# A batched matmul with scale and add: transposes moved from the matmul engine to three other engines, and a new order of transfers

## The chip, the cores and the metric

The kernel runs on one core of a Trainium2 chip. The metric is the device time of one execution in microseconds (us); the times shown are medians over several executions. One execution was also recorded by the hardware profiler: a page with summary tables and a trace of single instructions and transfers.

The engines are named as the profile names them: PE is TensorE (matmuls; PEld is its weight load), DVE is VectorE, ACT is ScalarE, POOL is GpSimd, SP is SyncE, which here only issues DMA transfers.

## The reference

```python
batch, m, k, n = 16, 512, 1024, 768
x: [16, 512, 1024] f32    weight: [1024, 768] f32    scale: 0.1    add_value: [16, 512, 768] f32
return (scale * np.matmul(x, weight) + add_value).astype(np.float32)
```

The batch is flattened: x has M = 8192 rows of K = 1024, the output 8192 rows of N = 768. The matmul is done in bf16 with f32 sums.

## The kernel before, in words

**Tiles.** The 8192 rows are cut into T = 64 tiles of 128 rows. Eight tiles form a group, so that one transfer brings several tiles at once in long runs: row p*8+t of a group is tile t, partition p. The weight (3.1 MB) is kept in SBUF as w_bf, 8 slices of 128 rows of K.

**Buffers.** x lands in xs, a ring of 16 tiles in f32. add_value lands in ao, a ring of 32 tiles; the result of a tile overwrites its addend there, and is sent out from there. The last eight slots of ao first hold the raw weight, and three below them the first three products until their addends come.

**The work on a tile.** The matmul needs x with K on the partitions, that is transposed. A tile is cast to bf16, and two neighbouring bf16 values are treated as one f32, so that four 128x128 f32 blocks are turned instead of eight. The rows of the weight are laid out to suit: slice 2c and 2c+1 hold the even and odd rows of a block. In the kernel before there are two ways to turn a tile:

- On PE (44 tiles): POOL casts the tile into an xb buffer (cast_to), PE turns the four blocks into PSUM (transpose, four matmuls with an identity), ACT copies them to an xt buffer in SBUF and separates even from odd.
- On DVE (20 tiles, the ten pairs of PAIRS): POOL casts both tiles of a pair into vx (cast_pair); DVE turns 32x32 blocks from one group of 32 partitions to another into vt (turn_pair), 16 instructions a pair, four after each of four steps.

Then product() issues 16 matmuls a tile: eight weight loads of 128x128 from the turned tile, each for 512 and for 256 columns. finish() on DVE multiplies by the scale, adds the addend and writes into ao.

**The order.** All is written out by hand; manual_schedule() keeps the order of the program on each engine. The list STREAM names the transfers in the order in which SP issues them: "x", "w" and "a" are loads, "o" stores; each entry has the first tile and the number of tiles. Ahead of a load into used slots of xs, or of a store, the program runs step() until the tiles concerned have been handed on. SP waits at each entry for the semaphores of what used the slots before, and later entries wait behind it. All transfers go through one queue to 16 DMA engines. In what follows x(16) means the entry that starts with tile 16 of x.

**The head.** The first three tiles are multiplied slice by slice as the weight arrives (head). Ten matmuls on zeros (WARM) are issued before.

**The steady state.** step() takes one tile t: its first eight matmuls, then the transposes of tile t+1 on PE, the cast of tile t+AHEAD, and the cast of a pair that starts at t+7; then the other eight matmuls, finish(t), and the DVE turns of the pair that starts up to six tiles ahead. The last tile is done in two parts, 512 columns and then 256.

Of the kernel before, what the change touches and what calls it, by code (L numbers as in the profile page):

```python
# [10 lines left out]

STREAM = [
# [6 lines left out]
]  # L19

X_SLOTS = 16
A_SLOTS = 32
AHEAD = 6
EARLY = 3
WARM = 10


PAIRS = [14, 19, 24, 29, 34, 39, 44, 49, 54, 59]


@with_exitstack
def kernel(
# [8 lines left out]
    nc = tc.nc  # L41
    P = 128
    bf16 = mybir.dt.bfloat16
    fp32 = mybir.dt.float32
# [4 lines left out]
    M, K = x_f.shape  # L49
    _, N = weight.shape  # L50
    T = M // P

    KC = K // (2 * P)
    KJ = 2 * KC
    CUT = 512
# [4 lines left out]
    out_v = out_f.rearrange("(g p t) n -> p g t n", p=P, t=G)  # L60

    def rows(view, s, n):
        assert s // G == (s + n - 1) // G
        return view[:, s // G, s % G:s % G + n, :]


    w_v = weight.rearrange("(c p r) n -> p c r n", p=P, r=2)

    const = ctx.enter_context(tc.tile_pool(name="const", bufs=1))
    xb_pool = ctx.enter_context(tc.tile_pool(name="xb_pool", bufs=7))  # L70
    xt_pool = ctx.enter_context(tc.tile_pool(name="xt_pool", bufs=EARLY + 1))
    vx_pool = ctx.enter_context(tc.tile_pool(name="vx_pool", bufs=1))
    vt_pool = ctx.enter_context(tc.tile_pool(name="vt_pool", bufs=2))
    tp_pool = ctx.enter_context(
        tc.tile_pool(name="tp_pool", bufs=2, space=bass.MemoryType.PSUM))
    mm_pool = ctx.enter_context(
        tc.tile_pool(name="mm_pool", bufs=3, space=bass.MemoryType.PSUM))
    ctx.enter_context(tc.manual_schedule())

    zeros = const.tile([P, CUT], bf16, name="zeros")  # L80
    nc.vector.memset(zeros, 0.0)  # L81
    identity = const.tile([P, P], fp32, name="identity")
    make_identity(nc, identity)
    xs = const.tile([P, X_SLOTS, K], fp32, name="xs")
    ao = const.tile([P, A_SLOTS, N], fp32, name="ao")
    w_bf = const.tile([P, KJ, N], bf16, name="w_bf")

    xb_tiles, xt_tiles, mm_tiles, done = {}, {}, {}, {"cast": 0, "step": 0, "x": 0}
    in_pair = {t0 + i: t0 for t0 in PAIRS for i in range(2)}
    vx_tiles, vt_tiles = {}, {}  # L90
    warm = mm_pool.tile([P, 1024], fp32, tag="mm")
    for _ in range(WARM):
        nc.tensor.matmul(warm[:, 0:CUT], zeros[:, 0:P], zeros, start=True, stop=True)  # L93

    def load_w(j, n):

        s = A_SLOTS - KJ + j
        if n == 1:
            nc.sync.dma_start(ao[:, s, :], w_v[:, j // 2, j % 2, :])
        else:  # L100
            nc.sync.dma_start(ao[:, s:s + 2, :], w_v[:, j // 2, :, :])  # L101
        for i in range(n):
            nc.vector.tensor_copy(w_bf[:, j + i, :], ao[:, s + i, :])  # L103

    def cast_pair(t0):
        vx = vx_pool.tile([P, 2, K], bf16, tag="vx")
        for i in range(2):
            nc.gpsimd.tensor_copy(vx[:, i, :], xs[:, (t0 + i) % X_SLOTS, :])  # L108
        vx_tiles[t0] = vx

    def turn_pair(t0, a):

        if a == 0:
            vt = vt_pool.tile([P, 2, KC, P], fp32, tag="vt")
            vt_tiles[t0] = vt
        pairs = vx_tiles[t0].bitcast(fp32).rearrange("p i (c k) -> p (i c) k", k=P)
        vt = vt_tiles[t0].rearrange("p i c m -> p (i c) m")
        for b in range(0, P, 32):
            nc.vector.transpose(  # L119
                vt[b:b + 32, :, 32 * a:32 * a + 32], pairs[32 * a:32 * a + 32, :, b:b + 32])  # L120

    def cast_to(t):
        while done["cast"] <= t:
            i = done["cast"]
            if i in in_pair:
                done["cast"] += 1
                continue
            xb = xb_pool.tile([P, K], bf16, tag="xb")
            src = xs[:, i % X_SLOTS, :]
            if i < EARLY:  # L130
                nc.vector.tensor_copy(xb[:, 0:K // 2], src[:, 0:K // 2])  # L131
                other = nc.gpsimd.tensor_copy if i else nc.scalar.copy
                other(xb[:, K // 2:K], src[:, K // 2:K])  # L133
            else:
                nc.gpsimd.tensor_copy(xb, src)  # L135
            xb_tiles[i] = xb
            done["cast"] += 1

    def transpose(t, pieces=1):
        cast_to(t)  # L140

        pairs = xb_tiles.pop(t).bitcast(fp32)
        tp = tp_pool.tile([P, KC, P], fp32, tag="tp")
        for c in range(KC):
            nc.tensor.transpose(tp[:, c, :], pairs[:, c * P:(c + 1) * P], identity)  # L145
        xt = xt_pool.tile([P, KJ, P], bf16, tag="xt")
        src = tp.bitcast(bf16).rearrange("p c (m r) -> p c r m", r=2)
        dst = xt.rearrange("p (c r) m -> p c r m", r=2)
        q = KC // pieces
        for c in range(0, KC, q):  # L150
            nc.scalar.copy(dst[:, c:c + q, :, :], src[:, c:c + q, :, :])  # L151
        xt_tiles[t] = xt

    def lhs(t, j):
        if t not in in_pair:
            return xt_tiles[t][:, j, :]
        t0 = in_pair[t]
        vt = vt_tiles[t0][:, t - t0, j // 2, :].bitcast(bf16)
        return vt.rearrange("p (m r) -> p r m", r=2)[:, j % 2, :]

    def product(t, j, cols):
        if (t, cols[0]) not in mm_tiles:
            mm = mm_pool.tile([P, 1024], fp32, tag="mm")
            for part in cols:
                mm_tiles[t, part] = mm
        for n0, n1 in cols:
            nc.tensor.matmul(  # L167
                mm_tiles[t, cols[0]][:, n0:n1], lhs(t, j), w_bf[:, j, n0:n1],
                start=(j == 0), stop=(j == KJ - 1))
# [3 lines left out]
    def finish(t, part, n0, n1):  # L173
        a = ao[:, t % A_SLOTS, n0:n1]
        nc.vector.scalar_tensor_tensor(  # L175
            a, mm_tiles[t, part][:, n0:n1], float(scale), a,
            op0=mybir.AluOpType.mult, op1=mybir.AluOpType.add)
# [32 lines left out]
    def step():  # L210
        t = done["step"]
        if t < T - 1:
            for j in range(KJ):
                if j == KJ // 2:
                    if t + 1 not in in_pair:
                        transpose(t + 1)
                    cast_to(min(t + AHEAD, done["x"] - 1))
                    if t + 7 in PAIRS:
                        cast_pair(t + 7)
                product(t, j, BOTH)  # L220
            finish(t, BOTH[0], 0, N)
            for a in range(P // 32):
                if t + 6 - a in PAIRS:
                    turn_pair(t + 6 - a, a)
        else:
            for cols in BOTH:
                for j in range(KJ):
                    product(t, j, [cols])
                finish(t, cols, *cols)
        done["step"] += 1  # L230

    def added(t):
        assert done["step"] >= EARLY
        nc.vector.tensor_add(  # L234
            ao[:, t, :], ao[:, EARLY_AT + t, :], ao[:, t, :])

    for op, s, n in STREAM:
        last = s + n - 1
        if op == "w":
            load_w(s, n)  # L240
            head(op, s, n)
        elif op == "x":
            if last >= X_SLOTS:
                while done["cast"] <= last - X_SLOTS:
                    step()
            k = s % X_SLOTS
            nc.sync.dma_start(xs[:, k:k + n, :], rows(x_v, s, n))  # L247
            done["x"] = s + n
            if last < EARLY:
                head(op, s, n)  # L250
        elif op == "a":
            k = s % A_SLOTS
            nc.sync.dma_start(ao[:, k:k + n, :], rows(add_v, s, n))
            for t in range(s, min(s + n, EARLY)):
                added(t)
        else:
            while done["step"] <= last:
                step()
            k = s % A_SLOTS
            nc.sync.dma_start(rows(out_v, s, n), ao[:, k:k + n, :])  # L260


# [33 lines left out]
```

## Time and profile before

| | before |
|---|---|
| median of 10 runs | 210.97 us (210.8 to 211.35) |
| the profiled execution | 211.01 us |
| its span, first to last instruction | 209.2 us |
| PE busy | 193.3 us, 92% |
| DVE busy | 138.2 us, 66% |
| POOL busy | 63.3 us, 30% |
| ACT busy | 47.2 us, 23% |
| moved by DMA | 87.21 MB, mean 417 GB/s |

The profile divides the span into 40 equal slices and gives the busy share of each engine in each, a digit for tenths, 9 for 90% or more. The DMA row is the mean share of the 16 DMA engines. Below that the page has the DMA queues (packets, MB, share of 16 engines): q1 carries the transfers of the program, q8 and q14 instructions. Groups of instructions are given by line of the kernel, engine and operation, with output<-input and shapes, the number of them, their busy time and the mean of one in ns, and then the idle time of the engine just ahead of them with what ended it. The list of transfers has the size and the median time from issue to landing.

### The profile page before, as it was taken

The page shows a single profiled execution, that of the slowest core. Times are in us where ns is not written, and L with a number is a line of the kernel's source. Part 1 is how long each engine was busy: PE and PEld are TensorE (multiplying, and loading weights), DVE is VectorE, ACT ScalarE, POOL GpSimd, SP SyncE. Part 2 cuts the span into 40 slices and gives each one's busy share as a digit, 9 for nine tenths or more (in the row PEclk, how much of TensorE's full clock was granted, in tenths as well). Part 3 has the DMA queues.
Part 4 walks back from the last instruction along what each step waited for, and adds up shares of the span by engine and source line. Part 5 has one row for each costly group of instructions (what it writes and reads, how often), then busy time and mean ns, then how long its engine had stood idle before and what let it go on. Part 6 is the DMA issues. An engine that isn't in the chain of part 4 may idle for free.

```text
span 209.2 us, 2949 instructions
## 1 busy us (share of the span) xinstructions
PE 193.3 (92%) x1187; PEld 117.8 (56%) x1210; DVE 138.2 (66%) x239; ACT 47.2 (23%) x50; POOL 63.3 (30%) x69
## 2 busy tenths in 40 slices
PE   7599499999899999999999999999999999999970
PEld 2355265665566566565666665565665666566630
DVE  0535533219969959998686986849994996973330
ACT  2513123323112113023031021130130320311210
POOL 1310524820292090503903607203603039100000
PEclk9979999999999999999999999999999999999998
DMA  6999999999999999999999999999999999999993
GB/s 230 419 427 440 427 422 429 453 449 407 418 460 417 418 432 423 428 445 421 437 435 426 440 420 417 437 424 432 418 446 429 457 407 418 437 431 437 409 395 154
DMA packets 4909, 87.21 MB, mean 417 GB/s; under 512 B 544, under 2 KB 544, under 8 KB 1312
## 3 DMA queue, kind: packets, MB, share of 16 engines
q1 hardware_dynamic: 4896, 87.03, 97.7%
q8 instruction: 9, 0.15, 0.3%
q14 instruction: 4, 0.03, 0.0%
HBM read 61.87 MB, written 25.17 MB: 416 GB/s over the span
## 4 chain that ended last, share of the span: by engine, by line
DMA 43%; PE 27%; DVE 13%; issue 7%; POOL 6%; SPq 1%; POOLq 0%; DVEq 0%
PE mm L167 25%; DMA xs<-in_x_dram 19%; DMA out_dram<-ao 15%; DVE vt L119 9%; DMA ao<-in_add_value_dram 8%; DVE ao L175 4%; POOL vx L108 3%; POOL xb L135 3%; PE tp L145 3%; SPq L101 1%; SPq L247 0%; POOLq L135 0%; DVEq L175 0%; POOLq L108 0%
## 5 line engine op out<-in xcount | busy, mean ns | idle before, releaser
L167 PE MATMUL mm<-w_bf,xt 128*128 128x512 bf16 (+1 forms) x687 | 122.5, 328 | 1.5 <-DVE ao L203 0.4
L167 PEld LDWEIGHTS <-xt 128*128 128x128 bf16 x704 | 66.2, 99 | 48.3 <-ACT xt L151 11.1
L175 DVE SCALAR_TENSOR_TENSOR ao<-mm,ao 128x768 f32<-128x768 f32 (+2 forms) x62 | 58.3, 944 | 43.6 <-PE mm L167 25.1
L151 ACT COPY xt<-tp 128x1024 bf16<-128x1024 bf16 (+1 forms) x47 | 44.6, 959 | 146.7 <-PE tp L145 146.7
L119 DVE STREAM_TRANSPOSE vt<-vx 32x256 f32<-32x256 f32 x160 | 69.7, 435 | 8.0 <-POOL vx L108 5.5
L135 POOL CAST xb<-xs 128x1024 bf16<-128x1024 f32 x41 | 41.4, 1043 | 55.4 <-DMA xs<-in_x_dram 55.4
L167 PE MATMUL mm<-w_bf,vt 128*128 128x256 bf16 (+1 forms) x314 | 54.7, 325 | 1.1 <-DVE vt L119 0.6
L167 PEld LDWEIGHTS <-vt 128*128 128x128 bf16 x320 | 31.1, 98 | 20.8 <-DVE vt L119 1.6
L108 POOL CAST vx<-xs 128x1024 bf16<-128x1024 f32 x20 | 20.3, 1040 | 53.5 <-DVE vt L119 43.9
L145 PE MATMUL tp<-identity,xb 128*128 128x128 f32 x176 | 26.8, 275 | 5.3 <-POOL xb L135 2.9
L145 PEld LDWEIGHTS tp<-identity,xb 128*128 128x128 f32 x176 | 20.5, 141 | 11.8 <-POOL xb L135 3.3
L103 DVE CAST w_bf<-ao 128x768 bf16<-128x768 f32 x8 | 4.1, 556 | 3.8 <-DMA ao<-in_weight_dram 3.8
L131 DVE CAST xb<-xs 128x512 bf16<-128x512 f32 x3 | 1.9, 696 | 5.9 <-DMA xs<-in_x_dram 5.9
L93 PE MATMUL warm<-zeros 128*128 128x512 bf16 x10 | 4.4, 632 | 1.2 <-DVE zeros L81 1.2
L203 DVE TENSOR_SCALAR ao<-mm 128x768 f32<-128x768 f32 x2 | 1.8, 954 | 2.5 <-PE mm L167 2.5
L133 POOL CAST xb<-xs 128x512 bf16<-128x512 f32 x2 | 1.6, 834 | 5.7 <-DMA xs<-in_x_dram 5.7
L93 PEld LDWEIGHTS <-zeros 128*128 128x128 bf16 x10 | 1.3, 144 | 3.4 <-issue 2.2
L234 DVE TENSOR_TENSOR ao<-ao 128x768 f32<-128x768 f32 x3 | 2.7, 951 | 0.0
L133 ACT CAST xb<-xs 128x512 bf16<-128x512 f32 x1 | 0.6, 618 | 5.0 <-DMA xs<-in_x_dram 5.0
L133 ACT ACT_TABLE_LOAD x1 | 1.3, 1283 | 0.7 <-PEq L277 0.7
L81 DVE MEMSET zeros<- 128x256 uint32 x1 | 0.3, 272 | 0.9 <-PEq L277 0.9
L200 ACT ACTIVATE ao<-mm 128x768 f32<-128x768 f32 x1 | 0.8, 817 | 0.0
(6 smaller groups left out, 0.9 us busy)
## 6 DMA issues: line engine op xcount, KB each, us to landing
xs<-in_x_dram SPq DMA_DIRECT2D x6, 4096.0 KB, 27.1
ao<-in_add_value_dram SPq DMA_DIRECT2D x7, 3072.0 KB, 24.3
out_dram<-ao SPq DMA_DIRECT2D x7, 3072.0 KB, 31.2
xs<-in_x_dram SPq DMA_DIRECT2D x3, 2048.0 KB, 25.4
ao<-in_weight_dram SPq DMA_DIRECT2D x4, 768.0 KB, 9.8
ao<-in_add_value_dram SPq DMA_DIRECT2D x1, 1920.0 KB, 21.0
xs<-in_x_dram SPq DMA_DIRECT2D x1, 1536.0 KB, 6.2
out_dram<-ao SPq DMA_DIRECT2D x1, 1536.0 KB, 12.9
```

What stands on the lines that cost most here:

```text
L93: nc.tensor.matmul(warm[:, 0:CUT], zeros[:, 0:P], zeros, start=True, stop=True)
L101: nc.sync.dma_start(ao[:, s:s + 2, :], w_v[:, j // 2, :, :])
L103: nc.vector.tensor_copy(w_bf[:, j + i, :], ao[:, s + i, :])
L108: nc.gpsimd.tensor_copy(vx[:, i, :], xs[:, (t0 + i) % X_SLOTS, :])
L119: nc.vector.transpose(vt[b:b + 32, :, 32 * a:32 * a + 32], pairs[32 * a:32 * a + 32, :, b:b + 32])
L133: other(xb[:, K // 2:K], src[:, K // 2:K])
L135: nc.gpsimd.tensor_copy(xb, src)
L145: nc.tensor.transpose(tp[:, c, :], pairs[:, c * P:(c + 1) * P], identity)
L151: nc.scalar.copy(dst[:, c:c + q, :, :], src[:, c:c + q, :, :])
L167: nc.tensor.matmul(mm_tiles[t, cols[0]][:, n0:n1], lhs(t, j), w_bf[:, j, n0:n1], start=(j == 0), stop=(j == KJ - 1))
L175: nc.vector.scalar_tensor_tensor(a, mm_tiles[t, part][:, n0:n1], float(scale), a, op0=mybir.AluOpType.mult, op1=mybir.AluOpType.add)
L234: nc.vector.tensor_add(ao[:, t, :], ao[:, EARLY_AT + t, :], ao[:, t, :])
```

## The change

- **Turning.** From tile 14 on no tile is turned on PE. Pairs of tiles go alternately to ACT (13 pairs, 14, 18, ... 62) and to POOL (12 pairs, 16, 20, ... 60). move_pair casts a pair from f32 to bf16 and in the same instruction moves 32 partitions to another group of 32: 16 instructions of 32 partitions x 512 elements a pair, four in each of four steps, starting eight tiles ahead. turn_moved is then one DVE instruction of 128x1024 f32, which turns each 32x32 block in its place, into an xt buffer of two tiles, four tiles ahead.
- Tiles 0 to 13 are still turned on PE. From tile 4 on DVE, not ACT, copies them out of PSUM; even and odd are no longer separated there, and product() reads its weights with a stride of two.
- **Buffers.** xb has 3 buffers (7 before), xt 3 of two tiles (4 of one), and the ACT and POOL moves have two each (va, vp). vx and vt go.
- **The head.** The ten matmuls on zeros go. The loads of w are written with another view of the same bytes.
- **Transfers.** 31 entries instead of 34. The head up to w(6) is the same; then add_value comes as a(0, 8) ahead of x(4), the order of the later loads and stores is another, and the last stores have 5 and 3 tiles instead of 4, 3 and 1.

```diff
 STREAM = [
     ("x", 0, 3), ("w", 0, 2), ("w", 2, 2), ("w", 4, 2), ("x", 3, 1), ("w", 6, 2),
-    ("a", 0, 3), ("x", 4, 4), ("a", 3, 5), ("x", 8, 4), ("x", 12, 4), ("a", 8, 8),
-    ("x", 16, 8), ("a", 16, 8), ("x", 24, 8), ("a", 24, 8), ("o", 0, 8), ("x", 32, 8),
-    ("a", 32, 8), ("x", 40, 8), ("o", 8, 8), ("x", 48, 8), ("a", 40, 8), ("o", 16, 8),
-    ("o", 24, 8), ("a", 48, 8), ("x", 56, 8), ("a", 56, 8), ("o", 32, 8), ("o", 40, 8),
-    ("o", 48, 8), ("o", 56, 4), ("o", 60, 3), ("o", 63, 1),
+    ("a", 0, 8), ("x", 4, 4), ("x", 8, 8), ("a", 8, 8), ("x", 16, 8), ("o", 0, 8),
+    ("a", 16, 8), ("x", 24, 8), ("x", 32, 8), ("a", 24, 8), ("a", 32, 8), ("x", 40, 8),
+    ("o", 8, 8), ("o", 16, 8), ("a", 40, 8), ("x", 48, 8), ("a", 48, 8), ("x", 56, 8),
+    ("o", 24, 8), ("o", 32, 8), ("a", 56, 8), ("o", 40, 8), ("o", 48, 8), ("o", 56, 5),
+    ("o", 61, 3),
 ]
...
-AHEAD = 6
+XB_BUFS = 3
+AHEAD = 4
 EARLY = 3
-WARM = 10
-PAIRS = [14, 19, 24, 29, 34, 39, 44, 49, 54, 59]
+MOVED_ACT = [14, 18, 22, 26, 30, 34, 38, 42, 46, 50, 54, 58, 62]
+MOVED_POOL = [16, 20, 24, 28, 32, 36, 40, 44, 48, 52, 56, 60]
...
-    warm = mm_pool.tile([P, 1024], fp32, tag="mm")
-    for _ in range(WARM):
-        nc.tensor.matmul(warm[:, 0:CUT], zeros[:, 0:P], zeros, start=True, stop=True)
...
-    def cast_pair(t0):
...
-    def turn_pair(t0, a):
...
+    def move_pair(t0, a):
+        act = t0 in MOVED_ACT
+        if a == 0:
+            if act:
+                va = va_pool.tile([P, 2 * KC, 4, 64], bf16, tag="va")
+            else:
+                va = vp_pool.tile([P, 2 * KC, 4, 64], bf16, tag="vp")
+            moved[t0] = va
+        k = t0 % X_SLOTS
+        assert k + 1 < X_SLOTS
+        src = xs[:, k:k + 2, :].rearrange("p i (c b k) -> p (i c) b k", b=4, k=64)
+        for b in range(4):
+            move = nc.scalar.copy if act else nc.gpsimd.tensor_copy
+            move(moved[t0][32 * b:32 * b + 32, :, a, :], src[32 * a:32 * a + 32, :, b, :])
+        if a == 3:
+            cast_pairs.add(t0)
+
+    def turn_moved(t0):
+        xt = xt_pool.tile([P, 2, KC, P], fp32, tag="xt")
+        for i in range(2):
+            xt_tiles[t0 + i] = xt[:, i, :, :]
+        nc.vector.transpose(
+            xt.rearrange("p i c m -> p (i c m)"),
+            moved.pop(t0).bitcast(fp32).rearrange("p c a k -> p (c a k)"))
...
+            if len(xb_tiles) == XB_BUFS:
+                break
...
-        xt = xt_pool.tile([P, KJ, P], bf16, tag="xt")
-        src = tp.bitcast(bf16).rearrange("p c (m r) -> p c r m", r=2)
-        dst = xt.rearrange("p (c r) m -> p c r m", r=2)
+        if t % 2 == 0:
+            xt = xt_pool.tile([P, 2, KC, P], fp32, tag="xt")
+            for i in range(2):
+                xt_tiles[t + i] = xt[:, i, :, :]
         q = KC // pieces
+        evacuate = nc.scalar.copy if t <= EARLY else nc.vector.tensor_copy
         for c in range(0, KC, q):
-            nc.scalar.copy(dst[:, c:c + q, :, :], src[:, c:c + q, :, :])
-        xt_tiles[t] = xt
+            evacuate(
+                xt_tiles[t][:, c:c + q, :].bitcast(bf16), tp[:, c:c + q, :].bitcast(bf16))
...
     def lhs(t, j):
+        xt = xt_tiles[t][:, j // 2, :].bitcast(bf16)
+        return xt.rearrange("p (m r) -> p r m", r=2)[:, j % 2, :]
...
-                    if t + 7 in PAIRS:
-                        cast_pair(t + 7)
+                    for a in range(4):
+                        if in_pair.get(t + 8 - a) == t + 8 - a:
+                            move_pair(t + 8 - a, a)
                 product(t, j, BOTH)
             finish(t, BOTH[0], 0, N)
-            for a in range(P // 32):
-                if t + 6 - a in PAIRS:
-                    turn_pair(t + 6 - a, a)
+            if in_pair.get(t + 4) == t + 4:
+                turn_moved(t + 4)
```

In the kernel after, the moves stand at line 117, the turn at line 125, the loads of x at line 256, of add_value at line 262 and the stores at line 270.

More of the change, by code (lines that the diff above doesn't have):

```diff
@@ L64, in rows @@
         return view[:, s // G, s % G:s % G + n, :]
-    w_v = weight.rearrange("(c p r) n -> p c r n", p=P, r=2)
+    w_v = weight.rearrange("(c p r) n -> p c (r n)", p=P, r=2)
     const = ctx.enter_context(tc.tile_pool(name="const", bufs=1))
[L70 to L73, printed above, removed]
+    xb_pool = ctx.enter_context(tc.tile_pool(name="xb_pool", bufs=XB_BUFS))
+    xt_pool = ctx.enter_context(tc.tile_pool(name="xt_pool", bufs=3))
+    va_pool = ctx.enter_context(tc.tile_pool(name="va_pool", bufs=2))
+    vp_pool = ctx.enter_context(tc.tile_pool(name="vp_pool", bufs=2))
     tp_pool = ctx.enter_context(
@@ L78 @@
     ctx.enter_context(tc.manual_schedule())
-    zeros = const.tile([P, CUT], bf16, name="zeros")
-    nc.vector.memset(zeros, 0.0)
     identity = const.tile([P, P], fp32, name="identity")
@@ L88 @@
     xb_tiles, xt_tiles, mm_tiles, done = {}, {}, {}, {"cast": 0, "step": 0, "x": 0}
-    in_pair = {t0 + i: t0 for t0 in PAIRS for i in range(2)}
-    vx_tiles, vt_tiles = {}, {}
-    warm = mm_pool.tile([P, 1024], fp32, tag="mm")
-    for _ in range(WARM):
-        nc.tensor.matmul(warm[:, 0:CUT], zeros[:, 0:P], zeros, start=True, stop=True)
+    in_pair = {t0 + i: t0 for t0 in MOVED_ACT + MOVED_POOL for i in range(2)}
+    moved, cast_pairs = {}, set()
     def load_w(j, n):
         s = A_SLOTS - KJ + j
[L98 to L101, printed above, removed]
+        assert j % 2 == n % 2 == 0
+        nc.sync.dma_start(
+            ao[:, s:s + n, :].rearrange("p (c r) n -> p c (r n)", r=2),
+            w_v[:, j // 2:(j + n) // 2, :])
@@ L102, in load_w @@
         for i in range(n):
             nc.vector.tensor_copy(w_bf[:, j + i, :], ao[:, s + i, :])
-    def cast_pair(t0):
-        vx = vx_pool.tile([P, 2, K], bf16, tag="vx")
-        for i in range(2):
-            nc.gpsimd.tensor_copy(vx[:, i, :], xs[:, (t0 + i) % X_SLOTS, :])
-        vx_tiles[t0] = vx
-    def turn_pair(t0, a):
[L113 to L120, printed above, removed]
+    def move_pair(t0, a):
[14 more added lines that the diff above has]
+            cast_pairs.add(t0)
@@ L125, in cast_to @@
             if i in in_pair:
+                assert in_pair[i] in cast_pairs
                 done["cast"] += 1
                 continue
+            if len(xb_tiles) == XB_BUFS:
+                break
             xb = xb_pool.tile([P, K], bf16, tag="xb")
@@ L145, in transpose @@
             nc.tensor.transpose(tp[:, c, :], pairs[:, c * P:(c + 1) * P], identity)
-        xt = xt_pool.tile([P, KJ, P], bf16, tag="xt")
-        src = tp.bitcast(bf16).rearrange("p c (m r) -> p c r m", r=2)
-        dst = xt.rearrange("p (c r) m -> p c r m", r=2)
+        if t % 2 == 0:
+            xt = xt_pool.tile([P, 2, KC, P], fp32, tag="xt")
+            for i in range(2):
+                xt_tiles[t + i] = xt[:, i, :, :]
         q = KC // pieces
+        evacuate = nc.scalar.copy if t <= EARLY else nc.vector.tensor_copy
         for c in range(0, KC, q):
-            nc.scalar.copy(dst[:, c:c + q, :, :], src[:, c:c + q, :, :])
-        xt_tiles[t] = xt
+            evacuate(
+                xt_tiles[t][:, c:c + q, :].bitcast(bf16), tp[:, c:c + q, :].bitcast(bf16))
     def lhs(t, j):
[L155 to L159, printed above, removed]
+        xt = xt_tiles[t][:, j // 2, :].bitcast(bf16)
+        return xt.rearrange("p (m r) -> p r m", r=2)[:, j % 2, :]
     def product(t, j, cols):
@@ L248 @@
             done["x"] = s + n
-            if last < EARLY:
+            if s < EARLY:
                 head(op, s, n)
@@ L259 @@
             k = s % A_SLOTS
-            nc.sync.dma_start(rows(out_v, s, n), ao[:, k:k + n, :])
+            n0, n1 = {"o": (0, N), "l": (0, CUT), "r": (CUT, N)}[op]
+            nc.sync.dma_start(rows(out_v, s, n)[:, :, n0:n1], ao[:, k:k + n, n0:n1])
 _INS = ['x', 'weight', 'scale', 'add_value']
```

## The prediction

> **What bounds the kernel now.** I read the page's parts 1 and 2 first. PE looks like the bound, and the DMA row under it says otherwise.
>
> ```profile
> PE 193.3 (92%) x1187; PEld 117.8 (56%) x1210; DVE 138.2 (66%) x239; ACT 47.2 (23%) x50; POOL 63.3 (30%) x69
> ...
> DMA  6999999999999999999999999999999999999993
> ...
> q1 hardware_dynamic: 4896, 87.03, 97.7%
> q8 instruction: 9, 0.15, 0.3%
> ```
>
> PE is busy for 92%, but the DMA engines are full in every slice but the first and last. The windows (PE, PEld, DVE, ACT, POOL busy; then PE clock, DMA share, GB/s) show how full:
>
> ```profile
> 30.00:60.00 30.00, 29.14 (x186) 18.02 (x189) 16.12 (x26) 8.10 (x8) 11.75 (x12) 1.00 1.01 430
> 150.00:180.00 30.00, 29.79 (x190) 18.36 (x192) 24.54 (x45) 6.32 (x7) 9.96 (x10) 1.00 1.00 431
> 195.00:200.00 5.00, 4.95 (x33) 3.08 (x33) 1.12 (x2) 2.02 (x2) 0.00 (x0) 1.00 0.98 420
> 203.00:206.00 3.00, 0.00 (x0) 0.00 (x0) 0.00 (x0) 0.00 (x0) 0.00 (x0) 1.00 0.92 382
> ```
>
> Both are at their limit, PE because its work nearly equals the DMA time. The packet records give the DMA rate: 32,768 bytes take 1.213 us on one of 16 engines, 27.0 bytes/ns, 432 GB/s together. 87.03 MB need 201.5 us; the first byte moves near 2 us. So no more than a few us can be won without moving fewer bytes, and the change moves the same 87.03 MB.
>
> Then I read the end: the timeline's last VectorE row, which ends at 202.9, and the page's last transfer, which it releases.
>
> ```profile
> 202.48 0.42 DVE L175 SCALAR_TENSOR_TENSOR ao<-mm,ao 128x256 f32<-128x256 f32 x1 [0.18 <-PE mm L167]
> ```
>
> ```profile
> out_dram<-ao SPq DMA_DIRECT2D x1, 384.0 KB, 5.3
> ```
>
> After 202.9 the last 0.39 MB takes 5.3 us where streaming needs 0.9, so it queues behind something. The landing records (16 per transfer, one per DMA engine) say what: first and last engine are 0.47 us apart at 27.5 us, 1.76 at 32.4, 2.13 at 182.9 and 3.56 at 190.2. The jumps follow the nine 16,384-byte packets of q8, at 28.5, 46.7, 67.5, 88.0, 106.2, 128.2, 148.5, 168.9 and 186.4 us. Each sets one engine back by about 1.3 us; as the landings tell, eight hit eight different engines and the ninth hits one again. A transfer lands with its slowest engine, so the end is that engine's: 208.23 us.
>
> [...]9 packets of 16,384 bytes, and between two of them PE starts 223 to 279 recorded instructions (250 on average, some records missing). [...]the 128x1024 casts of GpSimd take 1.04 us beside L119 and L175, but its two 128x512 casts at 7 us, beside VectorE's casts, took 0.86 and 0.80.[...]
>
> **The change part by part.** The durations:
>
> ```profile
> L135 POOL CAST xb<-xs 128x1024 bf16<-128x1024 f32 x41 | 41.4, 1043 | 55.4 <-DMA xs<-in_x_dram 55.4
> L119 DVE STREAM_TRANSPOSE vt<-vx 32x256 f32<-32x256 f32 x160 | 69.7, 435 | 8.0 <-POOL vx L108 5.5
> L133 ACT CAST xb<-xs 128x512 bf16<-128x512 f32 x1 | 0.6, 618 | 5.0 <-DMA xs<-in_x_dram 5.0
> L133 POOL CAST xb<-xs 128x512 bf16<-128x512 f32 x2 | 1.6, 834 | 5.7 <-DMA xs<-in_x_dram 5.7
> ```
>
> *PE.* A step is 16 matmuls, 2.63 us, and a transpose by PE 0.44 us (chain of waits). 44 tiles were transposed there, 14 remain: 30 x 0.44 = 13.2 us off. The 10 warm-up matmuls (4.4 us) ended before x0 landed at 7.0. PE's total falls to 64 x 2.63 + 14 x 0.44 = 174.5 us. None of it is on the path, as the DMA queue sets the pace: 1.31 MB a tile, 3.04 us. A slower PE clock in the head costs nothing while tile 4 is not there: a(0,8) now goes before x(4,4), which lands near 28 us instead of 23.4 (1.97 MB more ahead of it).
>
> *Instructions.* PE loses 20 for the warm-up and 30 x 8 for transposes, 260 of about 2,420, one refill's worth. In the trace the ninth refill came when PE had started 2,220. The new kernel has about 2,160. So the ninth goes, and with it the second hit on the slowest engine: at o(40) it landed 1.43 us later against the first engine. I take -1.43 us. The bounds are 0 (the refill stays, or 8 KB refills[...] fall on that engine; q14's four cost 0.36 to 0.66 each) and -1.8.
>
> *ScalarE and GpSimd.* Each pair of tiles takes 16 moves of 32 partitions x 512 elements, 4 per step. ScalarE does 13 pairs, GpSimd 12. ScalarE: 0.62 us by the 128x512 row[...]. GpSimd isn't shown alone at this size. Its casts follow each other every 0.984 us; half of that, 0.49, is the low end (no fixed cost), and 0.86,[...] the high end. [...]I take 0.60. That assumes neither quadrants nor 64-element runs cost more.
>
> What does a move's length decide? x(32) may start only when tiles 16 to 23 have left their slots. x(16) lands after 22.02 MB, as before, at 56.1 us; both engines then have 32 moves, so they end at 56.1 + 32 x 0.60 = 75.3 (ScalarE 75.9). Behind x(16) the queue holds o(0), a(16), x(24), 10.49 MB or 24.3 us. The fastest engine is through with x(16) near 53.9, so runs dry at 78.2; with 1.5 us from issue to first byte, x(32) must go by 76.7, for the slowest engine by 78.5. The limit is 0.64 to 0.70 us a move. x(40) stands the same behind x(32), a(24), a(32). x(48) and x(56) have over 10 us to spare. The other waits SP is queued behind, o(0) for step 7 and x(24) for tiles 8 to 15, are met 8 us ahead. So: no gap, by 1 to 3 us.
>
> *VectorE.* 160 transposes (69.7 us) go. 25 of 128x1024 come: [...]1.24 us, 31 us in all; and 10 copies out of PSUM, 1.0 us as ScalarE's or 1.2 at worst, 12 us. Each turn waits for moves issued a step before, and finish() is queued behind it; PE has 3 PSUM buffers, two steps of cover. It costs nothing unless moves fall behind. A move waits for the turn of two pairs back on its engine (va, vp hold two); only later moves are queued behind it. Strided weights cost nothing (98 ns for vt, 99 for xt), nor do three xb buffers instead of seven: GpSimd then casts one tile per step of 3 us, in 1.04, for tiles 4 to 13. Were that cover gone, it would be 1 us a tile on PE's path, ten times, against PE's 30 us of spare time. SP issues 31 transfers for 34, 0.4 us each, all while the queue is full.
>
> *The end.* a(56) lands after 77.6 MB, 179.6 + 5.4 = 185.0. Then finish(56), 1.0; PE, stopped with three tiles in PSUM, does steps 59 to 63, 13.2; finish 1.1: 200.3. o(61,3) is issued there; the fast engines run dry near 201.7, less 1.5 is 200.2. It just fits, and for the slow engine by 2 us.
>
> The sum: 208.23 - 1.43 = 206.8 for the last landing; the span ends 1.0 later as before, 207.8; outside the span lie 211.01 - 209.2 = 1.8. **209.6 us**, against 211.01 for the profiled execution, 0.04 above the median.
>
> **The rivals.**
> *A: the refill stays or its hit moves* (15%, small gaps at x(32) counted here). The DMA queue stays full and nothing is won: 210.6 to 211.3. For it: four q14 refills already fell on engines that I can't name.[...]
> *B: GpSimd becomes the bound* (33%, slower). If runs of 64 or changed quadrants cost it more, x(32) starves first at 0.64; above 0.70 its 192 moves run in one chain from x(16): 56.1 + 192d, then a turn 1.2, four steps 10.5, finish 1.1, o(61) 4.6, about 1.0 of waits: 74.5 + 192d. It passes 208.2 at d = 0.70, with the gap at x(32) at 0.67. d = 0.75 gives 218.5 + 2.8 = 221; the high end 0.86 gives 242. ScalarE, at 0.62 a move and with 13 pairs, has the same limit. For it: no such move is in the profile. Against: [...]0.49 by its halves.
> *C: PE was the bound* (2%). Then 13 us would go, 198. The full DMA rows exclude it.
> That the change does not do what it says would be transposes still on PE; the code leaves 14.
>
> **How the numbers follow.** The main case has 50%: 209.2 to 210.1. About 0.2%, 0.4 us, is what a measurement of this kernel can tell from no change. Faster is the main case and C, 0.52; within is nearly all of A, 0.13; slower is B and a rest of A, 0.35. The range reaches from 209.0 to B at d = 0.74: 219, and leaves out B's upper half.
>
> **What would show it.** Right: q8 with 8 packets, DMA rows of 9 to the end, POOL rows of L117 at 0.6 us, PE near 175 us busy with short gaps, the last transfer landing near 207 us. Wrong: L117 on POOL above 0.67 with SP waiting at L256 for it and 8s in the DMA row near 78 us; or q8 with 9 packets.

## The result and the profile after

| | before | after |
|---|---|---|
| median | 210.93 us (29 runs) | 214.24 us (213.66 to 214.75, 8 runs) |
| ratio to before | | 1.0153, 95% interval 1.0141 to 1.0165 |
| the profiled execution | 211.01 us | 213.46 us |
| its span | 209.2 us | 211.7 us |
| PE clock, mean | 0.988 | 0.964 |
| last landing | 208.22 us | 210.77 us |

The kernel after is 1.5% slower; the forecast was 209.6 us, faster. The profiled execution of after lies 0.8 us below its median, so the two traces can account for 2.45 us of the 3.3. A transfer lands when its data have arrived; the traces have 16 landings for each, one for each DMA engine.

The page of after, parts 1 to 3 (busy us, share of the span, instructions; then tenths in 40 slices; then packets, MB and share of 16 DMA engines), with the lines that answer to those of before:

```profile
PE 179.6 (85%) x1059; PEld 109.3 (52%) x1080; DVE 101.9 (48%) x113; ACT 134.8 (64%) x218; POOL 130.0 (61%) x211
...
DMA  6999999999899979999999999999999999999975
...
q1 hardware_dynamic: 4464, 87.03, 97.1%
q8 instruction: 8, 0.13, 0.2%
```

PE lost 13.7 us of work (the prediction had 18.8, from 193.3 to 174.5), and q8 has 8 packets for 9, as foreseen. But the DMA row has an 8 and a 7 at its 11th and 15th slice (52.9 to 58.2 and 74.1 to 79.4 us). In before the slices between the first and the last are all 9. The first dip is the change from x(16) to the first store, o(0), which no step of the prediction has; the second is where its rival B puts the first gap, the start of x(32). In the windows (PE, PEld, DVE, ACT, POOL busy, PE clock, DMA share, GB/s) of after:

```profile
75.00:80.00 5.00, 4.95 (x32) 2.96 (x31) 1.07 (x1) 2.02 (x4) 3.65 (x6) 1.00 0.78 311
80.00:85.00 5.00, 5.00 (x32) 3.03 (x32) 4.83 (x6) 3.40 (x6) 3.50 (x6) 1.00 0.94 374
110.00:120.00 10.00, 9.95 (x62) 6.07 (x62) 5.84 (x6) 9.80 (x17) 9.33 (x16) 1.00 1.00 416
170.00:180.00 10.00, 9.95 (x62) 6.04 (x62) 5.90 (x6) 9.80 (x17) 9.33 (x16) 1.00 1.00 430
```

Around 80 us the DMA engines move 311 and 374 GB/s; in the steady state they are full (1.00 of the time, 416 and 430 GB/s). PE is at 4.95 of 5.00 in the gap too: it still works on what landed before. The gap is paid at the end, since the bytes that were not moved at 80 us are moved after all others.

The costliest groups (busy us, mean ns of one | idle before, and its releaser) of after, for the durations:

```profile
L117 ACT CAST va<-xs 32x512 bf16<-32x512 f32 x208 | 128.1, 616 | 41.8 <-DMA xs<-in_x_dram 39.3
...
L117 POOL CAST va<-xs 32x512 bf16<-32x512 f32 x192 | 116.5, 607 | 26.5 <-DMA xs<-in_x_dram 18.1
...
L125 DVE STREAM_TRANSPOSE xt<-va 128x1024 f32<-128x1024 f32 x25 | 30.9, 1235 | 44.9 <-POOL va L117 44.9
...
L163 DVE COPY xt<-tp 128x1024 bf16<-128x1024 bf16 x10 | 6.9, 688 | 13.3 <-PE tp L155 13.3
```

All four are within 2% of the prediction or below it (0.62, 0.60, 1.24, 1.0 us). The 0.60 was an estimate, between the 0.49 and 0.86 that the prediction takes from the trace of before. The 1.24 was an estimate too; another, from the slope of finish() in before (425, 692 and 957 ns for 256, 512 and 768 columns, 1.04 ns a column), is 435 ns for the turn of 256 columns and 768 x 1.04 more, 1.23 us. A single duration is not what went wrong. The timeline of POOL in after, from the landing of x(16) (start us, us from the first start to the last end of a run of equal instructions), and that of ACT under it:

```profile
57.00 2.55 POOL L117 CAST va<-xs 32x512 bf16<-32x512 f32 x4 [9.19 <-DMA xs<-in_x_dram]
59.62 1.03 POOL L145 CAST xb<-xs 128x1024 bf16<-128x1024 f32 x1
60.72 18.18 POOL L117 CAST va<-xs 32x512 bf16<-32x512 f32 x28
```

```profile
56.97 20.08 ACT L117 CAST va<-xs 32x512 bf16<-32x512 f32 x32 [8.16 <-DMA xs<-in_x_dram]
```

And the timeline of SP in after, with x(32) in before under it:

```profile
60.68 18.57 SPq L256 DMA_DIRECT2D xs<-in_x_dram  x2
79.30 0.90 SPq L262 DMA_DIRECT2D ao<-in_add_value_dram  x2
102.09 0.33 SPq L256 DMA_DIRECT2D xs<-in_x_dram  x1
102.46 0.91 SPq L270 DMA_DIRECT2D out_dram<-ao  x2
```

```profile
64.20 0.33 SPq L247 DMA_DIRECT2D xs<-in_x_dram  x1
```

The 28 moves end at 60.72 + 18.18 = 78.90, and the second of the two loads at L256, x(32), is issued at 78.92 by the trace, the loads of add_value behind it at 79.30. The fastest DMA engine had been dry (had finished all that was issued) since 78.37. In before x(32) was issued 21.5 us before the fastest engine had done what stood ahead of it.

**A ledger.** For each transfer the landing records of the trace have a time for each DMA engine. From the landing of the slowest engine I take off the time that the bytes moved so far need at 432 GB/s; what is left is its lost time, with some 3.3 us of start in it, and it rises only where time is lost (another engine can be the slowest at the next transfer). Below, a step is such a rise, and a refill is one of the 16,384-byte packets of q8, which the page calls instruction. Between two of them PE starts 250 recorded instructions on average in after (215 to 274), as in before.

| lost time of the slowest engine, us, after the transfer | before | after |
|---|---|---|
| x(4) | 3.68 | 3.58 |
| x(8), with a refill (at 28.5 us in before, 35.5 in after) | 5.05 | 4.78 |
| the load ahead of o(0): a(24) in before, x(16) in after | 5.22 (no step) | 5.98 (+1.2) |
| x(32) | 5.19 | 8.64 (+2.7) |
| x(40) | 5.20 | 9.39 (+0.75) |
| o(40), with the ninth refill in before | 6.81 (+1.4) | 9.36 (none) |
| the last | 6.76 | 9.31 |

The last row differs by 2.55 us, as the landings do. The ninth refill is gone as forecast, -1.4; a step ahead of o(0) that the prediction doesn't have takes +1.2 of that back; x(32) and x(40) cost 3.45. The experiments ask of each of these whether it is a cause.

While the queue is full, the packets of one engine follow each other within some 15 ns, so that each engine can be followed through the packet records. In before, eight refills fall on eight engines and the ninth, at 186.4 us, on the one that had the first, at 28.5 us, as the prediction read from the landings; each holds up its engine's other packets by 1.4 to 1.55 us.

### The profile page after: what moved, and what is told of

Same layout as the page of the kernel before. It is cut to its first block, busy times and chain, and to the rows that moved or that the text cites. A ratio compares the mean times of both kernels' runs of the same rounds, so it can differ in the third digit from the quotient of the medians.

```text
span 211.7 us, 2844 instructions
## 1 busy us (share of the span) xinstructions
PE 179.6 (85%) x1059; PEld 109.3 (52%) x1080; DVE 101.9 (48%) x113; ACT 134.8 (64%) x218; POOL 130.0 (61%) x211
## 4 chain that ended last, share of the span: by engine, by line
DMA 43%; PE 29%; POOL 16%; issue 7%; SPq 2%; DVE 1%; POOLq 0%; DVEq 0%
DMA xs<-in_x_dram 32%; PE mm L176 27%; POOL va L117 15%; DMA out_dram<-ao 11%; PE tp L155 2%; POOL xb L145 1%; SPq L96 1%; DVE ao L184 1%; SPq L256 1%; SPq L262 0%; POOLq L145 0%; POOLq L117 0%; DVE xt L125 0%; DVEq L184 0%
## 5 line engine op out<-in xcount | busy, mean ns | idle before, releaser
L176 PE MATMUL mm<-w_bf,xt 128*128 128x512 bf16 (+1 forms) x1003 | 172.9, 331 | 8.8 <-DVE ao L184 7.1
L117 ACT CAST va<-xs 32x512 bf16<-32x512 f32 x208 | 128.1, 616 | 41.8 <-DMA xs<-in_x_dram 39.3
L176 PEld LDWEIGHTS <-xt 128*128 128x128 bf16 x1024 | 102.0, 100 | 76.6 <-issue 6.3
L117 POOL CAST va<-xs 32x512 bf16<-32x512 f32 x192 | 116.5, 607 | 26.5 <-DMA xs<-in_x_dram 18.1
L125 DVE STREAM_TRANSPOSE xt<-va 128x1024 f32<-128x1024 f32 x25 | 30.9, 1235 | 44.9 <-POOL va L117 44.9
L145 POOL CAST xb<-xs 128x1024 bf16<-128x1024 f32 x11 | 11.2, 1040 | 29.2 <-DMA xs<-in_x_dram 18.4
L155 PE MATMUL tp<-identity,xb 128*128 128x128 f32 x56 | 10.2, 318 | 17.6 <-POOL xb L145 9.8
L155 PEld LDWEIGHTS tp<-identity,xb 128*128 128x128 f32 x56 | 7.6, 163 | 19.8 <-POOL xb L145 10.6
L163 DVE COPY xt<-tp 128x1024 bf16<-128x1024 bf16 x10 | 6.9, 688 | 13.3 <-PE tp L155 13.3
L163 ACT COPY xt<-tp 128x512 bf16<-128x512 bf16 (+1 forms) x7 | 4.1, 656 | 8.2 <-PE tp L155 8.2
```

What stands on the lines that cost most here:

```text
L117: move(moved[t0][32 * b:32 * b + 32, :, a, :], src[32 * a:32 * a + 32, :, b, :])
L125: nc.vector.transpose(xt.rearrange("p i c m -> p (i c m)"), moved.pop(t0).bitcast(fp32).rearrange("p c a k -> p (c a k)"))
L163: evacuate(xt_tiles[t][:, c:c + q, :].bitcast(bf16), tp[:, c:c + q, :].bitcast(bf16))
L176: nc.tensor.matmul(mm_tiles[t, cols[0]][:, n0:n1], lhs(t, j), w_bf[:, j, n0:n1], start=(j == 0), stop=(j == KJ - 1))
```

## The experiments

Theory 1: the late x(32), and after it x(40), is the loss. Theory 2: the moves themselves slow something else, such as PE's clock (0.964 against 0.988) or VectorE. Each ratio is to runs of before made beside the kernel; kernels that ran together share them.

### Another transfer in the place of the late one (e1_order, e2_a24_only)

```diff
-    ("a", 16, 8), ("x", 24, 8), ("x", 32, 8), ("a", 24, 8), ("a", 32, 8), ("x", 40, 8),
-    ("o", 8, 8), ("o", 16, 8), ...
+    ("a", 16, 8), ("x", 24, 8), ("a", 24, 8), ("x", 32, 8), ("a", 32, 8), ("o", 8, 8),
+    ("x", 40, 8), ("o", 16, 8), ...
```

> Only two entries of the list of transfers move: a(24) ahead of x(32), o(8) ahead of x(40); 3.1 MB more stand before each of the two loads. Theory 1 (GpSimd's chain of moves hands the slots of xs back too late, so the queue runs dry before x(32), and nearly so before x(40)): both gaps go, and with them 2.7 + 0.75 us of the last landing: 210.2 to 211.3 us. Theory 2 (the loss lies in what the 400 moves do to the other engines and the DMA, or in PE's lower mean clock, 0.964 for 0.988, wherever the loads stand): 213.5 to 214.6 us, with the gap gone and the time not.

Measured: 210.69 us (210.04 to 211.01, 12 runs), ratio 0.9979 (0.9968 to 0.9989). The DMA row of its page, and its windows at x(32) and x(40):

```profile
DMA  6999999999999999999999999999999999999975
```

```profile
75.00:80.00 5.00, 4.95 (x31) 3.01 (x31) 0.79 (x1) 2.30 (x4) 3.92 (x7) 1.00 0.92 393
80.00:85.00 5.00, 5.00 (x33) 3.03 (x32) 5.00 (x6) 3.08 (x5) 3.18 (x6) 1.00 1.05 452
101.00:106.00 5.00, 4.95 (x32) 2.99 (x31) 3.59 (x4) 4.89 (x9) 4.64 (x9) 1.00 0.93 398
```

Two pairs of entries swapped win back 3.5 us. x(32) is issued no earlier (79.21 us; it was 78.92), but a(24), which waits for nothing at that time, now fills the 7.3 us ahead of it. The lost time of the slowest engine stays at 6.2 to 6.3 us through x(32) and x(40). The moves are all still there, and PE's mean clock is 0.958, lower than in after: theory 2 is out.

The second kernel makes only the first swap.

> Only a(24) moves ahead of x(32). Theory 1: x(32) is in time, but x(40) still has 24.3 us of queue behind x(24) and needs 32 moves at 0.65, 20.8 us, and a start of 2 to 3 us. The gap moves to x(40) and the time stays: 213.3 to 214.6 us. If x(32) alone is late for a cause of its own (the cast of tile 13, the refill just before x(16) lands), x(40) stays in time: 211 to 211.8. Theory 2: 213.5 to 214.6, but with no gap before x(40).

Measured: 213.56 us (213.07 to 214.1, 4 runs), ratio 1.0121 (1.0098 to 1.0144). Its windows:

```profile
75.00:80.00 5.00, 4.95 (x32) 3.05 (x32) 0.91 (x1) 2.18 (x4) 3.79 (x7) 1.00 0.92 390
80.00:85.00 5.00, 5.00 (x32) 2.94 (x31) 4.98 (x6) 3.19 (x6) 3.29 (x6) 1.00 1.03 442
101.00:106.00 5.00, 4.95 (x32) 2.95 (x31) 3.70 (x4) 4.89 (x9) 4.68 (x8) 1.00 0.88 326
```

At 80 us nothing is lost any more, and at 101 to 106 us the queue runs thin instead: x(40) is issued at 102.29 us, 0.36 us before the fastest engine is dry, because the transfers ahead of it are no longer late. It costs the slowest engine 2.7 us (6.14 to 8.85), as x(32) did before. A stall that is taken away uncovers the next late transfer: the first swap alone brings 0.7 us by the medians, both together 3.5.

### The same moves, started earlier (e3_halves)

```diff
-    ..., ("x", 16, 8), ("o", 0, 8), ("a", 16, 8), ("x", 24, 8), ("x", 32, 8), ...
+    ..., ("x", 16, 4), ("x", 20, 4), ("o", 0, 8), ("a", 16, 8), ("x", 24, 4), ("x", 28, 4), ("x", 32, 8), ...
```

> The order is that of the change, but x(16) and x(24) come as two loads of 4 tiles each, so that the moves of the first pairs start about 4.9 us earlier. Theory 1: the moves end at 74 and 98 us instead of 79 and 102, no gap, 210.2 to 211.5 us. Theory 2, or a place in the order that is bad by itself: 213.5 to 214.6 us.

Measured: 210.78 us (210.36 to 211.54, 15 runs), ratio 0.9993 (0.9983 to 1.0002). The timeline of SP in it shows what changes: x(32), the third of these three loads, goes at 72.96 us, and x(40) at 97.62.

```profile
47.87 25.42 SPq L256 DMA_DIRECT2D xs<-in_x_dram  x3
73.34 1.56 SPq L262 DMA_DIRECT2D ao<-in_add_value_dram  x2
97.62 0.33 SPq L256 DMA_DIRECT2D xs<-in_x_dram  x1
```

Here the order of after is kept, x(32) still ahead of a(24); the moves only begin with the first half of the eight tiles. The lost time stays between 6.2 and 6.5 us to the end. A second cure of another kind gives the same time: what cost 3.5 us was the late issue.

### Four moves more (e4_more)

```diff
         if a == 3:
+            if t0 == 20:
+                for b in range(4):
+                    nc.gpsimd.tensor_copy(
+                        moved[t0][32 * b:32 * b + 32, :, a, :], src[32 * a:32 * a + 32, :, b, :])
             cast_pairs.add(t0)
```

> The last four moves of pair 20 on GpSimd are done twice (the same values again): 4 x 0.65 = 2.6 us more in the chain ahead of x(32), nothing else. Theory 1: x(32) goes out 2.6 us later, at about 81.5, and the end moves by all of it: 216.4 to 217.2 us. Theory 2: GpSimd has 80 us idle in all, so 214.2 as before.

Measured: 216.19 us (215.86 to 216.65, 4 runs), ratio 1.0247 (1.0226 to 1.0267), 1.95 us above after by the medians and 3.2 by the profiled executions, and 0.2 us below the range expected. Its windows:

```profile
75.00:80.00 5.00, 4.95 (x32) 3.04 (x31) 0.00 (x0) 2.15 (x4) 4.57 (x9) 1.00 0.61 259
80.00:85.00 5.00, 2.42 (x13) 1.14 (x11) 3.21 (x4) 3.28 (x6) 4.65 (x8) 0.89 0.56 179
```

x(32) goes at 81.78 us, 2.86 later for four moves 0.67 apart. The fast engines lose all of that more than in after (5.1 us at x(32) for 2.2). Of the 3.2 us of the slowest one only 0.8 stand at x(32), 1.7 at the two loads behind a(24), a(32) and x(40), and 0.4 at o(32), for which I have no cause. So more work in GpSimd's queue ahead of x(32) makes the whole kernel longer, by the medians by two thirds of its own size; in this kernel even PE runs empty (2.42 of 5.00).

### Each half of the change alone (e5_order_alone, e6_moves_alone)

The first is the kernel before with the new STREAM, the second the kernel after with the old one.

> The kernel before, with nothing changed but its list of transfers, which is that of the change. PE still turns 44 tiles (44 x 0.44 us), and tile 4 is there 4.5 us later, as a(0) goes ahead of x(4). If the order needs the lighter PE: PE ends near 208 us instead of 202.5, the stores of the last 8 tiles start late, 214.5 to 218 us. If the order alone is harmless and the moves are the fault: 210.5 to 212.

Measured: 216.89 us (216.81 to 217.12, 4 runs), ratio 1.0280 (1.0266 to 1.0293). The page and the windows of its end:

```profile
DMA  7999999999999999999999999999999999997355
```

```profile
195.00:200.00 5.00, 5.00 (x34) 3.19 (x33) 1.91 (x2) 0.17 (x1) 0.00 (x0) 1.00 0.59 251
200.00:205.00 5.00, 5.00 (x34) 2.96 (x32) 1.82 (x2) 1.85 (x2) 0.00 (x0) 1.00 0.49 206
205.00:210.00 5.00, 4.81 (x32) 2.76 (x29) 1.91 (x4) 1.01 (x1) 0.00 (x0) 1.00 0.46 197
```

No gap anywhere, but at the end PE is full and the DMA engines wait for it at half load. The new order brings x(4) at 27.68 us instead of 23.40, and a PE that still transposes 44 tiles doesn't make up for that: up to 4.3 us of the 6 can be this. For the rest the trace shows PE waiting 2.5 us for VectorE's turns and finish(), where it waits 0.6 in before, and a granted clock of 0.96 between 30 and 60 us (1.00 in before); no run separates these. In after PE has the 13 us for it.

> The change with the list of transfers of the kernel before: the moves alone. The theory of the late slots: x(32) now has 31.6 us of queue behind x(16) and is in time, but x(48) has only a(32), x(40) and o(8), 24.3 us, behind x(32) and must wait for 32 moves, 20.8 us on GpSimd, and a start of 2 to 3 us: the gap of 1 to 3 us stands before x(48) instead, 212 to 215.5 us. If the new order alone is at fault: 210 to 211.

Measured: 215.03 us (214.87 to 217.41, three runs; a fourth took 218.2), ratio 1.0225 (1.0181 to 1.0269). The old order was not made for the time at which the moves free the slots. The trace is of the execution of 217.41 us. x(24) goes at 59.69 us (43.24 before), x(48) at 120.79 (114.01), and the lost time of the slowest engine goes from 5.0 to 7.66 at a(24) and from 7.64 to 10.67 by a(40). The last stores are late as well: o(60) goes at 209.51 us. So each half loses alone, and together they lose less than either.

### The ninth refill given back (e8_fill100, e9_fill20)

Both start from e1_order and add small matmuls of unused results at the end of the head; 100 of them bring the ninth refill back, 20 don't.

```diff
+            fill = mm_pool.tile([P, 1024], fp32, tag="mm")
+            for _ in range(FILL):
+                nc.tensor.matmul(
+                    fill[:, 0:64], w_bf[:, 0, 0:P], w_bf[:, 0, 0:64], start=True, stop=True)
```

> The two moved entries of the run with a(24) and o(8) ahead (210.69 us), and 100 small matmuls (128x64, results unused) on PE while it waits for tile 4: about 200 more PE instructions. Theory of refills: a ninth 16 KB packet on q8, all others earlier; the end is 87.03 MB at 432 GB/s plus what the refills on the slowest engine cost it: with one hit on it 209.3, with two 210.7, with three 212 us, and the landing records show the steps of 1.2 to 1.4 us at the refills. If refills do not matter: 210.7 and no such steps, whatever their number.

> As the run before, with 20 small matmuls, about 40 more PE instructions: still eight refills, each earlier by 40 instructions, some 3 us. Theory of refills: 209.3, 210.7 or 212 us by the number of hits on the slowest engine (one, two, three), steps in the landing records at the refills; if which engine is hit depends on the moment of the refill, it can change from the two hits, near 36 and 56 us, seen without the matmuls. If refills do not matter: 210.7.

Measured: with 100, 211.84 us (211.16 to 212.15, 12 runs), ratio 1.0037 (1.0026 to 1.0048), and the page's row of q8 has nine packets:

```profile
q8 instruction: 9, 0.15, 0.3%
```

With 20, 210.45 us (210.05 to 211.44, 20 runs), ratio 0.9976 (0.9968 to 0.9984), eight packets. The difference, 1.4 us to the kernel with 20 and 1.15 to e1_order, is near what the prediction gave the refill (1.43). The last landings of the two traces don't show it (208.47 us with 100, 208.76 with 20), but the profiled execution was the shortest of the first kernel's runs and the longest of the second's. The packet records do show how it comes about. With 20, the eight refills fall on eight engines. With 100, the ninth, at 191.2 us, falls on the engine that had the first, at 23.9 us, and makes it the slowest; the landing of o(40) is 0.9 us later for it. In the trace with 20 the slowest engine loses 0.8 us at a(56), where no refill falls on it. The two kernels also differ by 80 small matmuls, and that these cost nothing is not shown.

### The step ahead of o(0) (e10_o0_behind_a16, e11_o0_behind_a24)

In after, e1 to e5, e8 and e9 the slowest engine loses 1.1 to 1.5 us in the last packets of x(16) (in e3 of its second half, x(20)), the load just ahead of the first store; the kernel before shows no such step. Both kernels start from e1_order and put o(0) further back.

```diff
-    ..., ("x", 16, 8), ("o", 0, 8), ("a", 16, 8), ("x", 24, 8), ("a", 24, 8), ("x", 32, 8), ...
+    ..., ("x", 16, 8), ("a", 16, 8), ("o", 0, 8), ("x", 24, 8), ("a", 24, 8), ("x", 32, 8), ...   # e10
+    ..., ("x", 16, 8), ("a", 16, 8), ("x", 24, 8), ("a", 24, 8), ("o", 0, 8), ("x", 32, 8), ...   # e11
```

> The run with a(24) and o(8) ahead (210.69 us), and o(0) one place later, behind a(16). In that run, as in all with the new order, every engine's last packet of x(16), near 52.5 us, takes 1.3 to 1.8 us instead of 1.21, and the slowest engine's 2.7: a step of 1.4 us in the landing of x(16). Theory of the switch (the step comes where the first store follows x(16) directly): no step at x(16), 209.1 to 209.7 us. Theory of refills (the second refill, near 56 us, hit the slowest engine): unchanged, 210.4 to 211.

> The same, with o(0) behind a(24), where the kernel before has it: the order x(16), a(16), x(24), a(24), o(0), x(32) is then that of the kernel before. Theory of the switch: no step at x(16), 209.1 to 209.7 us. Theory of refills: 210.4 to 211. x(32) has 31.6 us of queue behind x(16) in both cases and is in time.

Measured: e10 210.27 us (210.12 to 210.66, 5 runs), ratio 0.9964 (0.995 to 0.9978); e11 211.26 us (210.8 to 212.38, 17 runs), ratio 1.0021 (1.0008 to 1.0034). In e10 x(16) lands without a step (5.00 us lost), and a(16), now the load ahead of o(0), has it: 5.00 to 6.23. So the step went with o(0), and was not avoided. It is not the refill that comes near x(16) either (56.0 us in after, 55.6 in e10). In after that refill falls on its engine behind x(16), in o(0). In e10 it falls on one engine early in a(16), but the last two packets of a(16) are slow on an engine that has no refill there as well (1.3 us lost). Neither time is in the range of the theory of the switch. In e11 the slowest engine loses 1.75 us at a(24), ahead of o(0); but there x(24) was issued at 59.70 us, 1.3 us before the fastest engine was dry, and the fastest engine loses 1.0 us at a(24) as well (0.2 to 0.4 in the step of the others). That loss may be x(24)'s; e11 doesn't decide, and its time is above both ranges.

e10 has the lowest median of all. x(16) lands 1 us earlier, so x(32) goes 1 us earlier (77.94); the trace ends with the last landing at 207.98 us.

### The kernel before with a late first store (e12_o0_late_58, e13_o0_late_50)

One thing that tells before from after is when o(0) is issued: 8 us ahead of its turn in after, 14.5 in e10, 34 in before. Two kernels change only that in the kernel before (LATE is 12 in e12, 9 in e13).

```diff
-            while done["step"] <= last:
+            while done["step"] <= (LATE if s == 0 else last):
                 step()
+            if s == 0:
+                nc.vector.tensor_copy(ao[:, 0, 0:1], ao[:, 0, 0:1])
```

> The kernel before with its order of transfers untouched; a one-column VectorE copy of tile 0 onto itself after step 12, which o(0) waits for, makes SP issue o(0) near 58.5 us instead of 44.15, some 20 us ahead of the end of a(24) instead of 34.5. x(32), behind it on SP, is not held by that (64.2 us). Theory L (a store whose issue comes late in the loads ahead of it slows the last packets of those loads): the slowest engine's offset at a(24) goes from 5.22 to 6.4 to 6.9 and the time to about 212.2 us, the step that the kernel after shows ahead of o(0). Rival: the step belongs to other things that differ between before and after (length of the other queue entries, the load of ScalarE and GpSimd), then the offset at a(24) stays near 5.2 and the time near 210.95.

> The same with the copy after step 9: o(0) is issued near 50.2 us, 28.5 us ahead of the end of a(24). By theory L, if there is a limit of lead between 20 and 34.5 us, this run says on which side 28.5 lies: time about 212.2 us with an offset above 6.4 at a(24), or 210.95 with 5.2. If e12 shows no step either, this one shows none.

Measured: e12 210.88 us (210.4 to 211.87, 22 runs), ratio 0.9998 (0.9989 to 1.0006); e13 210.93 us (210.52 to 211.34, 14 runs), ratio 0.9992 (0.9984 to 1.0001). o(0) is issued at 58.59 and 52.01 us, and a(24) shows no step (5.21 and 5.12 us lost). So theory L fails for these leads: one of 19.6 us makes no step. A limit between 14.5 and 19.6 us would still fit all kernels but e11 and e6, where x(24) is late as well; so would the place of o(0), which in all kernels without a step stands behind a(24). That stays open.

## Why the prediction was wrong

**The step that failed** is "So: no gap, by 1 to 3 us" at x(32). It stood on an end of the moves at 75.3 us, and they ended at 78.9. Three terms of that sum were mis-sized:

1. The moves: 32 x 0.60. One takes 0.607, but the next starts only 0.649 after (18.18 / 28): the price of an instruction was right, that of a row of them was not. 32 x 0.049 = 1.6 us. ScalarE, 0.628 apart, was done at 77.05; GpSimd held SP.
2. The cast of tile 13, which the code has in GpSimd's queue between the moves, was left out: 1.1 us with its gaps. The prediction counts these casts for GpSimd's own time in tiles 4 to 13, and not where they stand in the queue.
3. x(16) lands at 56.95 us and not at 56.1, by the step ahead of o(0): 0.85 us.

Together 3.6 us, against a margin of 1 to 3. e4 shows that more work in that queue makes the kernel longer, e1 and e3 that without the wait the 3.5 us are not lost. The spacing alone, 32 x 0.649 from 56.1, would have ended the moves at 76.9, only 0.2 us beyond the 76.7 that the prediction names for the fastest engine; it takes the other two terms to make 78.9.

**Also mis-sized** was what a late issue costs the slowest engine. x(32) went 2.2 us later than the 76.7 that the prediction allows the fastest engine, and the fast ones lost 2.2 us by the landings: 0.55 dry until the issue, 1.0 from the issue to the first byte (the prediction has 1.5; in before the first 16 packets, of a transfer issued at 0.73 us, begin between 1.74 and 2.19 us, 1.0 to 1.5 after), and about 0.8 in first packets of 2.0 us for 1.213. For the slowest engine it allows 78.5, so that 0.4 should have been lost, and the landings show 2.7. By the packet records one engine begins x(32) only at 82.16 us, 3.2 after the issue, and its first packet takes 2.60 us. Which engine it is can't be told across the gap, and why it is late is open. x(40), which the prediction says "stands the same", was issued 2.7 us before the fastest engine was dry and still cost 0.75.

**Rival B** came true in its mild form: GpSimd holds x(32), at that place, for the queue's sake and not for a slower instruction. It had a third of the chance; its price here is 3.45 us.

**The end** is a second step that failed, and after hides it. The sum has PE stopped with three tiles in PSUM until a(56) lands, and o(61,3) issued 15.3 us behind that landing. It went 17.5 us behind it, at 206.49. PE was not stopped for a(56): it works without a wait from 162.83 us to its end at 206. It had stopped before, for 4.8 us, because finish() stood in VectorE's queue behind a turn that waited for GpSimd's moves. The prediction put this wait at nothing "unless moves fall behind". In after:

```profile
DVE xt L125 <- POOL va L117: 44.9, 12, 9.4
PE mm L176 <- DVE ao L184: 7.1, 3, 4.8
```

(who waited for whom: us in all, times, the longest.) It costs after next to nothing, as the slowest DMA engine was busy with o(56) until 207.7, when the others had just begun o(61). But in e1, where the gaps are closed, 15 engines land o(61) by 207.71 us and the slowest one at 208.21: without its steps e1 would have ended 0.5 us earlier and no more (an estimate from these landings).

**What held.** The DMA queue sets the time (e1's full row; PE's 13.7 us brought nothing). The ninth refill went, and one more refill costs 1.15 to 1.4 us by the medians of e8, e1 and e9. But the -1.43 didn't come through: in e1 the step ahead of o(0), which no line of the sum has, took 1.4, and a smaller one at a(56) 0.6. So e1, with every gap closed, is 0.2% below before and not 0.7%. VectorE's turns (30.9 us) and the copies out of PSUM (6.9 us) cost the time nothing by the same row. The late x(4) costs nothing with the lighter PE, and e5 shows that this cover is needed.

## What to carry to other kernels

In a kernel bound by its DMA queue the question about a slower way off the critical engine is not how busy the engines are (GpSimd 61% in after), but when the last instruction of the slowest one frees the buffer of the next transfer (78.90 us for x(32)): add up everything in that engine's queue, other work included, by the spacing of instructions in a row and not by the duration of one (0.649 and 0.607 us here). In e1 and e3, 5.1 to 7.6 us between the issue and the time at which the fastest DMA engine is dry were enough, and 2.7 in after were not (5 in e4 leave it open). Where such a lead is not to be had, put a transfer that waits for nothing ahead of the one that may be late (3.5 us in e1). After such a swap look for the next late transfer before judging it (x(40) in e2, 2.7 us).

## What the runs showed that I had not expected

- GpSimd's moves of 32x512 follow each other with a gap (0.607 long, 0.649 apart), while its casts of 128x1024 in before start every 0.984 us though each is given 1.04. Half the spacing of the long ones, 0.49, is no price for a short one.
- How far ahead a load of x was issued, and what it lost on the fastest engine: 0.55 us after that engine was dry, 2.2 us (x(32) in after); 0.36 us before, 2.4 (x(40) in e2); 2.7 before, 0.65 (x(40) in after); 5.1 and 5.4 before, 0.1 or less (e3); 6 and more before (e1), nothing. In e4 x(40) was issued 5 us before, and the fastest engine still lost 0.8; what of that is the issue's I can't say.
- A step of 1.1 to 1.5 us on the slowest engine in the last packets ahead of the first store, in every kernel with o(0) behind x(16) or a(16), with the moves and without (e5), and in none of the three with o(0) behind a(24) and x(24) issued early (before, e12, e13). Its cause is open.
